# Splitting the feed-forward's first gate slabs anew in each block instead of storing the parts

## Chip, cores, metric

The kernel runs on one core of a Trainium2 chip. The metric is the device time of one execution in microseconds (us), median of several runs.

## What is computed

One layer of a hybrid encoder, in float32, for a prompt of 2048 tokens and a sample of 64 tokens (2112 rows), with a model width of 1024. The change sits between the last residual of the attention part and the feed-forward:

```python
x = x + gt1 * (merged @ p['w_o'])

h2 = rms_norm(x, p['norm2_g']) * (1 + sc2) + sh2
gate, up = jnp.split(h2 @ p['w_ffn_in'], 2, axis=-1)
x = x + gt2 * ((jax.nn.silu(gate) * up) @ p['w_ffn_out'])
```

Before it stand an adaLN-conditioned norm, one input projection, a convolution module and band attention in parallel, and their gated merge. The hidden width of the feed-forward is 2816, 22 slices f of 128.

## The kernel before, in words

**Precision.** Each float32 factor of a product is split into a high part, rounded to the reduced format fp32r, and a low part, the rest. A product is three matmuls: high by high, high by low, low by high. For a weight slab ScalarE (ACT) makes the high part by a copy into `whi`, and VectorE (DVE) or GpSimd (POOL) the low part `wlo` by a subtraction.

**Stages.** The tokens go through the feed-forward in three blocks s = 0, 1, 2 of 576, 768 and 768 rows (`CBLOCKS`). Each is worked in two halves of 288 or 384 rows. In each block, merge (`ca` slabs) and output projection (`wo` slabs) come first; then, tile by tile of 128 tokens, the residual: VectorE forms `x`, ACT its sum of squares (`xn<-x`, the "square"), POOL `r`, the reciprocal root, ACT scales (`xn<-x,r`), TensorE (PE) transposes (`pw<-ident,xn`), and ACT and DVE apply the conditioning and make the operands of the feed-forward: `b` (b11, b21, b22), sums `t` (t1 to t4), each with a high and a low part. The feed-forward's products are arranged in a Strassen-like scheme: some operands are sums of slices of the weights (`s1` to `s4`, made on POOL from raw slabs as `ws`, and kept in DRAM as `sum_d` for the later blocks), others are the raw slices. Several products `early` and `tg` are taken ahead of time.

**The slabs of the change.** The keys `("fi", f*P)` for the first five f (`EARLY = 5`) are raw gate slabs of 128 x 8 x 128, 512 KB each. They feed the first products of the first half (`first(f)` and `second(f)`, lines 2216 to 2240; `ps<-b,whi` in the profile), which TensorE starts while the other tiles are still in the residual: 24 products each, 120 in all. In block 0 the raw slab is loaded (`load`, L375) into a staging buffer (`wst`, three; `wup`, one more) and split in two parts of 4 x 128 columns (`split`, L451): the copies on ACT, the subtractions on VectorE for odd f and on POOL for even f (`turn`). After the split, `then` stores both parts to DRAM (`w_dfi_h`, `w_dfi_l`, L501). In blocks 1 and 2 nothing is split: `split` finds the key in `self.stored` and loads both parts straight into `whi` and `wlo` (L466). Five buffers of each (`held`) go round among all slabs.

**What sets the order.** Each engine works through its own queue in the order of issue. A planner (`stream`) writes that order as the program is built: work is put in lanes with estimated loads of the engines, and a step that has become due is issued where the estimate says so. Loads go out on SyncE's queue (SP) as staging buffers come free by the same estimate (`load_on`, `drop`); sums are formed when their raw slabs should have landed (`presum`). So an edit to one slab can move others' places in the queues.

The order of slabs (lines 584 to 608): per block `ca` and `wo` for each half, then the five `fi`, then pairs of sums and raw slices (`up`), and the down projection's (`dn`, `fo`).

Of the kernel before, what the change touches and what calls it, by code (L numbers as in the profile page):

```python
# [57 lines left out]
SCORE_ROOM = {"dve": 2500}  # L58
TURN_NS = 600.0
POOL_BEHIND = 3000.0  # L60
KEPT = ("qkv", "in", "fi")
EARLY = 5


# [519 lines left out]
def weight_order():  # L584
    yield from (("qkv", 0, k) for k in range(4))
    for b, stage in ORDER:
        if stage == "g":
            for g in range(0, 16, 2):
                yield from (("in", 2560 + g * P, h) for h in range(2))
        elif stage in ("q", "k", "v"):  # L590
            if b or stage != "q":
                yield from (("qkv", "qkv".index(stage), k) for k in range(4))
        else:
            yield from (("in", CONV + stage * P), ("in", stage * P))
    for s in range(len(CBLOCKS)):
        for _ in range(2):
            yield from (("ca", c) for c in range(KT))
            yield from (("wo", k) for k in range(KT))
        yield from (("fi", f * P) for f in range(EARLY))
        for f in range(0, NF, 2):  # L600
            ops = up_operands(f) + up_operands(f + 1)
            for j in range(0, len(ops), 2):
                yield ("up", *ops[j : j + 2])
                if f >= 2 and seven(s, f - 2):
                    yield from (("dn", s, f - 2, *DOWN_OPERANDS[i]) for i in {0: (0,), 2: (1, 2), 4: (3,)}.get(j, ()))
                elif j == 0 and f >= 2 and f - 2 not in last_rows(s):
                    yield from (("fo", f - 2), ("fo", f - 1))
        yield from (("fo", f) for f in last_rows(s))
# [3 lines left out]
def streaming_layer(ctx: ExitStack, tc: tile.TileContext, I, O):  # L612
# [294 lines left out]
    def first_rows():  # L907
        places = ((wa, "x", 3), (wa, "x", 3), (wa, "x", 3), (wk, "kk", 1), (wk, "q2", 1))
        queues = (nc.sync, nc.sync, nc.scalar, nc.sync, nc.scalar)
        return [load_x(*tl, *place, q) for tl, place, q in zip(token_tiles(*PBLOCKS[0]), places, queues)]  # L910
# [691 lines left out]
    xs = first_rows()  # L1602
    W = Weights((nc.sync, act, dve, gps), wpool, dram, stream, list(weight_order()), source, 3, 5, lambda key: key[0] in KEPT)
    first_block(xs)
# [692 lines left out]
```

## Time and profile before

| | |
|---|---|
| median of 3 runs | 2979.57 us (2976.84 to 2982.91) |
| the profiled execution | 2979.5 us |
| its span | 2977.7 us |
| mean granted TensorE clock | 0.995 |
| PE busy | 2900.2 us (97%) |
| DVE busy | 2025.9 us (68%) |
| ACT busy | 1356.8 us (46%) |
| POOL busy | 1127.7 us (38%) |
| DMA | 628.05 MB, 211 GB/s on average |

The profile is of one execution, and its times are us from the span's start. A row of the timeline gives the start, the length, the engine, the line of the code, the operation, the tile written and the tiles read, the size, and in brackets how long the engine had stood idle before it and on whose result. A row of groups gives the count, the summed busy time, the mean in ns, and the idle time before. Starts that follow each other by less than the length of the first belong to operations that overlap in the engine's pipeline. Nearly all compute instructions carry L102, a helper that records them, so they are told apart by their tiles. The feed-forward of block 0 begins near 1307 us, of block 1 near 1851 us, of block 2 near 2480 us.

### The profile page before, as it was taken

The numbers are of one execution on the slowest core, as the hardware profiler recorded it, in microseconds if no ns is written. First come the engines' busy times: TensorE is split into PE (matmuls) and PEld (weight loads), VectorE is DVE, ScalarE is ACT, GpSimd is POOL, SyncE is SP. The second block draws the span as 40 slices with busy tenths as digits, with TensorE's granted clock in tenths as the row PEclk, the third lists the DMA queues.
The fourth block names the chain that finished last, engine by engine and source line by source line (L and its number), as shares of the span: only waits on it lengthen the run. The fifth ranks groups of instructions, "written<-read, shape, count | busy, mean of one in ns | idle before, by whom it ended". The sixth has DMA issues, their size and how long they took to land.

```text
span 2977.7 us, 44838 instructions
## 1 busy us (share of the span) xinstructions
PE 2900.2 (97%) x16199; PEld 2593.1 (87%) x16199; DVE 2025.9 (68%) x3637; ACT 1356.8 (46%) x2441; POOL 1127.7 (38%) x727
## 2 busy tenths in 40 slices
PE   7999899999999999989999999999999999999999
PEld 4899777787888888888999999999999999999998
DVE  5797677767856886577777755666666557466666
ACT  2345642662456257464444345534444345344442
POOL 0201310111011102454466443255666741465667
PEclk9999999999999999999999999999999999999999
DMA  8889889878987798885444786333333975333333
GB/s 290 300 286 310 270 279 312 284 251 274 306 283 224 267 263 278 262 288 175 145 145 159 244 263 235 116 95 106 114 113 113 316 239 184 93 95 114 114 103 128
DMA packets 467723, 628.05 MB, mean 211 GB/s; under 512 B 36276, under 2 KB 314664, under 8 KB 467501
## 3 DMA queue, kind: packets, MB, share of 16 engines
q1 hardware_dynamic: 453456, 605.58, 62.8%
q10 hardware_dynamic: 14045, 19.60, 1.9%
q8 instruction: 127, 2.08, 0.3%
q14 instruction: 95, 0.78, 0.1%
HBM read 476.53 MB, written 148.54 MB: 210 GB/s over the span
## 4 chain that ended last, share of the span: by engine, by line
PE 82%; DVE 7%; DMA 4%; ACT 2%; issue 2%; POOL 2%; SPq 0%; ACTq 0%; POOLq 0%; DVEq 0%
PE ps L102 53%; PE pd L102 16%; PE pw L102 6%; DVE y L102 2%; PE sc L102 2%; PE po L102 2%; PE ptp L102 2%; DVE wlo L102 1%; PE pt L102 1%; DMA kk<-k_d 1%; ACT whi L102 1%; PE pa L102 1%; POOL r L102 1%; DVE pw L102 1%; DMA wst<-in_w_in 0%
## 5 line engine op out<-in xcount | busy, mean ns | idle before, releaser
L102 PE MATMUL ps<-t,whi 128*128 128x384 f32 (+1 forms) x2112 | 503.1, 322 | 8.7 <-ACT t L102 4.9
L102 POOL TENSOR_TENSOR wlo<-wst,whi 128x1024 fp32r<-128x1024 f32 (+1 forms) x156 | 356.4, 2294 | 279.0 <-ACT whi L102 262.6
L102 ACT ACTIVATE whi<-wst 128x1024 fp32r<-128x1024 f32 (+1 forms) x263 | 256.8, 979 | 331.2 <-PE ps L102 119.8
L102 PE MATMUL ps<-b,whi 128*128 128x384 f32 (+1 forms) x1584 | 381.7, 326 | 7.0 <-DVE early L102 3.6
L102 PEld LDWEIGHTS ps<-t,whi 128*128 128x128 f32 x2112 | 367.8, 188 | 16.3 <-ACT t L102 5.1
L102 DVE SCALAR_TENSOR_TENSOR y<-u,wd,y 128x512 f32<-128x512 f32 (+1 forms) x480 | 369.0, 773 | 6.3
L102 PE MATMUL ps<-hh,whi 128*128 128x512 f32 (+2 forms) x992 | 361.7, 365 | 0.0
L102 DVE TENSOR_TENSOR acc<-acc,pd 128x512 f32<-128x512 f32 x464 | 311.7, 685 | 62.7 <-PE pd L102 60.2
L102 PE MATMUL ps<-hl,whi 128*128 128x512 f32 (+2 forms) x992 | 345.6, 348 | 0.0
L102 PE MATMUL ps<-hh,wlo 128*128 128x512 f32 (+2 forms) x992 | 345.4, 348 | 0.0
L102 PE MATMUL ps<-t,wlo 128*128 128x384 f32 (+1 forms) x1056 | 339.4, 322 | 0.8 <-POOL wlo L102 0.7
L102 PE MATMUL pd<-whi,hid 128*128 128x512 f32 x972 | 314.8, 390 | 0.0
L102 PEld LDWEIGHTS ps<-b,whi 128*128 128x128 f32 x1584 | 278.7, 189 | 13.1 <-DVE early L102 4.5
L102 POOL TENSOR_TENSOR r<-t,mhalf 128x1 f32<-128x1 f32 (+3 forms) x68 | 83.6, 1232 | 462.1 <-DVE t L102 457.0
L102 PE MATMUL ps<-b,wlo 128*128 128x384 f32 (+1 forms) x792 | 257.3, 325 | 0.0
L102 ACT ACTIVATE pr<-pr,sm 128x640 f32<-128x640 f32 (+3 forms) x272 | 200.1, 747 | 112.1 <-DVE sm L102 109.5
L102 PEld LDWEIGHTS pd<-whi,hid 128*128 128x128 f32 x972 | 182.5, 188 | 37.7 <-ACT hid L102 0.7
L102 PEld LDWEIGHTS ps<-hh,wlo 128*128 128x128 f32 x992 | 186.7, 188 | 21.6
L102 PEld LDWEIGHTS ps<-hh,whi 128*128 128x128 f32 x992 | 187.2, 189 | 18.5 <-issue 1.6
L102 PEld LDWEIGHTS ps<-hl,whi 128*128 128x128 f32 x992 | 187.5, 189 | 15.5 <-issue 1.4
L102 PEld LDWEIGHTS ps<-t,wlo 128*128 128x128 f32 x1056 | 198.2, 188 | 2.2 <-POOL wlo L102 1.3
L102 PE MATMUL pd<-wlo,hid 128*128 128x512 f32 x508 | 198.6, 391 | 0.0
(226 smaller groups left out, 6170.6 us busy)
## 6 DMA issues: line engine op xcount, KB each, us to landing
whi<-w_din_h SPq DMA_DIRECT2D x72, 512.0 KB, 6.5
wlo<-w_din_l SPq DMA_DIRECT2D x72, 512.0 KB, 8.4
wst<-sum_d SPq DMA_DIRECT2D x132, 256.0 KB, 2.7
wfo<-in_w_ffn_out SPq DMA_DIRECT2D x64, 512.0 KB, 3.2
wmod<-in_w_ada SPq DMA_DIRECT2D x46, 512.0 KB, 6.5
sum_d<-ws SPq DMA_DIRECT2D x88, 256.0 KB, 2.8
wst<-in_w_ffn_in SPq DMA_DIRECT2D x84, 256.0 KB, 3.1
wst<-in_w_in SPq DMA_DIRECT2D x40, 512.0 KB, 8.8
```

The lines of the kernel that those rows point to most:

```text
L102: self.last = f(*args, **kw)
```

## The change

`KEPT` names the kinds of slabs whose split parts are stored in DRAM at their first use and loaded again afterwards. `fi` is taken off the list. In block 0 the ten stores (five high, five low parts) go. In blocks 1 and 2 each `fi` slab is loaded raw into a staging buffer and split there as in block 0. The planner makes the orders of the queues anew.

```diff
@@ -58,7 +58,7 @@
 SCORE_ROOM = {"dve": 2500}
 TURN_NS = 600.0
 POOL_BEHIND = 3000.0
-KEPT = ("qkv", "in", "fi")
+KEPT = ("qkv", "in")
 EARLY = 5
```

The lines that it switches:

```python
W = Weights((nc.sync, act, dve, gps), wpool, dram, stream, list(weight_order()), source, 3, 5, lambda key: key[0] in KEPT)
...
if key in self.again and key not in self.stored and not passing:
    ds = [self.dram.tile(shape, F32, name="w_d" + "_".join(map(str, key)) + "_" + part) for part in "hl"]
    for t, d in zip((hi, lo), ds):
        self.sync.dma_start(d, t.bitcast(F32))
    self.stored[key] = ds, shape
```

## Prediction

> **What bounds the kernel now.** I read the page first, then its times by stage, then single instructions where the change acts. Of the page, the busy times and the chain that ended last:
>
> ```profile
> PE 2900.2 (97%) x16199; PEld 2593.1 (87%) x16199; DVE 2025.9 (68%) x3637; ACT 1356.8 (46%) x2441; POOL 1127.7 (38%) x727
> PE 82%; DVE 7%; DMA 4%; ACT 2%; issue 2%; POOL 2%; SPq 0%; ACTq 0%; POOLq 0%; DVEq 0%
> ```
>
> TensorE has 77.5 of 2977.7 us free, so a microsecond in which it newly waits is a microsecond of time, and none is made good later. The shares say little of the change, which acts at three places only: where each token block goes from its residual into the feed-forward. The table of stretches (us, then busy PE, PEld, DVE, ACT, POOL, PE clock, DMA share, GB/s) shows them for block 1, and one row of block 2:
>
> ```profile
> 1820.00:1840.00 20.00, 20.00 (x90) 16.58 (x89) 3.61 (x5) 3.18 (x3) 3.57 (x2) 1.00 0.48 159
> 1840.00:1860.00 20.00, 19.84 (x105) 17.64 (x105) 14.81 (x30) 13.45 (x28) 1.65 (x3) 1.00 0.72 261
> 1860.00:1880.00 20.00, 19.20 (x111) 18.48 (x110) 19.97 (x33) 14.89 (x27) 5.81 (x2) 1.00 0.33 113
> 2490.00:2510.00 20.00, 19.29 (x111) 18.89 (x112) 19.31 (x31) 13.85 (x25) 5.70 (x2) 1.00 0.33 108
> ```
>
> Over the whole run VectorE is busy 68%; from 1860 to 1880 it is busy 19.97 of 20 us, and TensorE is still 96% busy. There the two are level. That is the stage that prices the change, and it has no room on VectorE. Before 1840 all the helpers are nearly idle, and work that can move there is free. TensorE loses only 0.96 us in the two windows 1840 to 1880, so blocks 1 and 2 can win about 2 us together and no more.
>
> **What the change takes away.** All moves of the split slabs stand on SP's queue:
>
> ```profile
> L466 SPq DMA_DIRECT2D whi<-w_dfi_h x10: 319/383/498, 1834.3 to 2480.2; - x10
> L501 SPq DMA_DIRECT2D w_dfi_h<-whi x5: 531/1115/3045, 1298.8 to 1317.9; - x5
> ```
>
> With the low parts there are 10 stores in block 0 and 10 loads in each of blocks 1 and 2, each 512 KB. The stores go; the 20 loads become 10 loads of raw slabs, so SP issues 20 DMAs fewer. In blocks 1 and 2 DMA is at 0.33 to 0.72, and no wait of TensorE there hangs on a load; the saved bytes are worth nothing there.
>
> **What it adds.** In blocks 1 and 2 each of five slabs is split in two halves of 512 columns: ten ACT copies per block, four subtractions on VectorE (slabs 1 and 3), six on GpSimd (slabs 0, 2, 4). Block 0 already does this work, and gives the durations:
>
> ```profile
> L102 ACT ACTIVATE whi<-wst 128x512 fp32r<-128x512 f32 x50 | 30.9, 625 | 24.2 <-issue 18.2 <-POOL wlo L102 2.9 <-PE ps L102 2.9
> L102 DVE TENSOR_TENSOR wlo<-wst,whi 128x512 fp32r<-128x512 f32 x28 | 33.0, 1185 | 7.9 <-ACT whi L102 7.0 <-PE ps L102 0.5
> L102 POOL TENSOR_TENSOR wlo<-wst,whi 128x512 fp32r<-128x512 f32 x22 | 33.1, 1505 | 6.9 <-ACT whi L102 6.9
> ```
>
> So 10 x 0.63 = 6.3 us on ACT, 6 x 1.5 = 9.0 on GpSimd, 4 x 1.19 = 4.7 on VectorE at these means. VectorE's mean is raised by neighbours: alone the operation takes 0.68, beside a running GpSimd sum 1.76. GpSimd's own shortest of this size is near 1.27.
>
> ```profile
> 1333.07 0.68 DVE L102 TENSOR_TENSOR wlo<-wst,whi 128x512 fp32r<-128x512 f32 x1
> 1342.93 1.76 DVE L102 TENSOR_TENSOR wlo<-ws,whi 128x512 fp32r<-128x512 f32 x1
> 1327.91 1.27 POOL L102 TENSOR_TENSOR ws<-wst 128x512 f32<-128x512 f32 x1 [10.48 <-DVE t L102]
> ```
>
> [...]
>
> What part is on the path follows from the built order of the changed program, which is the same in blocks 1 and 2. ACT has slab 0's two copies ahead of tile 0's square (there it sat idle 10.33 us: free, and so are GpSimd's two halves). Then come slabs 1 to 4, mixed into the work on the three token tiles of the residual: slabs 3 and 4 between the square of tile 1 and its scaling. GpSimd has the four halves of slabs 2 and 4 ahead of the small r (root of the mean square) of tiles 1 and 2. VectorE has slab 1 and 3 amid tile 0's columns. In the timeline of block 1 before:
>
> ```profile
> 1841.48 1.06 ACT L102 ACTIVATE xn<-x 128x1024 f32<-128x1024 f32 x1 [10.33 <-DVE x L102]
> 1848.01 1.07 ACT L102 ACTIVATE xn<-x 128x1024 f32<-128x1024 f32 x1
> 1849.43 0.55 POOL L102 TENSOR_TENSOR r<-t,mhalf 128x1 f32<-128x1 f32 x1 [5.99 <-DVE t L102]
> 1850.01 1.16 ACT L102 ACTIVATE xn<-x,r 128x1024 f32<-128x1024 f32 x1 [0.50 <-POOL r L102]
> 1851.13 0.52 PE L102 MATMUL ps<-b,whi 128*128 128x384 f32 x2
> 1851.66 0.52 PE L102 MATMUL ps<-b,whi 128*128 128x384 f32 x2
> 1853.26 1.03 PE L102 MATMUL pw<-ident,xn 128*128 128x128 f32 x8
> 1854.05 0.60 PE L102 MATMUL ps<-b,whi 128*128 128x384 f32 x2
> 1863.77 1.04 PE L102 MATMUL pw<-ident,xn 128*128 128x128 f32 x8
> 1875.24 0.52 PE L102 MATMUL ps<-t,whi 128*128 128x384 f32 x2
> ```
>
> Step 1, the norm of tile 1. Back to back an ACT copy takes some 0.5 (0.63 less an overlap of 0.1). Four more (slabs 1 and 2) stand ahead of the square, which goes from 1848.0 to 1850.0 and ends at 1851.1; slab 4's buffer, the one of the last output-projection slab, comes free just then, at 1851.13. Four copies more (slabs 3 and 4) end near 1853.1. GpSimd's two halves of slab 4 follow the copies, from 1852.6, and at 1.27 each end near 1855.4 with the hand-over; r comes at 1856 instead of 1849.98, 6.0 later. Tile 1 is scaled by 1857.2 instead of 1851.2.
>
> Step 2, TensorE. Before, tile 1 was transposed at 1853.26, after 12 of the 120 gate products, and tile 2 at 1863.77, after 60; in the built order after, both stand behind the 60th. A product takes (1851.66 - 1851.13) / 3 = 0.177, so 60 take 10.6; with an estimated 0.8 of waits for the gate banks they end at 1862.55, the transposes (1854.05 - 1853.26 = 0.8 a tile) at 1864.15, and the other 60 at 1874.8. The delay of r is thus mostly hidden on TensorE itself: it does products meanwhile. What isn't hidden is VectorE, which had done tile 1's columns in that time.
>
> Step 3, VectorE.
>
> ```profile
> 1847.81 0.41 DVE L102 TENSOR_SCALAR xn<-pw,A,B 128x128 f32<-128x128 f32 x1 [0.61 <-ACT xn L102]
> 1867.97 0.68 DVE L102 TENSOR_TENSOR pw<-pw,b 128x512 f32<-128x512 f32 x1
> 1868.57 0.40 DVE L102 TENSOR_SCALAR pw<-pw,A,B 128x128 f32<-128x128 f32 x1
> 1868.89 0.39 DVE L102 TENSOR_SCALAR xn<-pw,A,B 128x128 f32<-128x128 f32 x1
> 1874.24 0.68 DVE L102 TENSOR_TENSOR t<-pw,t 128x512 fp32r<-128x512 f32 x1
> 1874.83 1.22 DVE L102 TENSOR_TENSOR wlo<-wup,whi 128x1024 fp32r<-128x1024 f32 x1
> 1875.97 0.69 DVE L102 TENSOR_TENSOR pw<-xn,pw 128x512 f32<-128x512 f32 x1
> 1881.27 0.56 DVE L102 TENSOR_TENSOR u<-ps,early 128x384 f32<-128x384 f32 x1 [0.76 <-PE ps L102]
> ```
>
> From start to start an operation of 512 columns takes 0.60, one of 128 columns 0.32, a subtraction of 1024 columns 1.14. After the first transposes (1863.35) the built order has 14 of 512 and 6 of 128 up to the last tile's t3: 10.3 us. The columns go to and fro with ACT; the wait of 0.61 shows such a hand-over, and I allow four or five, 2.7. The t3 is ready at 1876.4, which TensorE wants at 1874.8: 1.6 late, where it came in time before. From there to u, whose end frees the bank for the next products, stand 9 of 512, two of 1024, and three gate operations (0.46, the 0.56 of u less 0.1 of overlap): 9.1 us, so u starts at 1885.5, against 1881.27: 4.2 late. In between TensorE has 24 products and 12 more (6.4 us), which, with 0.8 of waiting for the next t, last until 1883.6; then it waits some 2.3 for u. I take 4.2 us per block.
>
> Bounds of a block: below, -1 (the waits TensorE has now); 0 if VectorE's idle takes the halves up; 1.6 if only the t3 wait shows. Above, the delay of r passed on whole (6.0) with 2.4 of halves, 8.4. I take 4.2 because it lies nearest to VectorE's own rows, which leave it no idle in this stretch.
>
> **Block 0.** TensorE stands three times here, and after the first two the clock is low:
>
> ```profile
> 1318.72 0.73 PE L102 MATMUL ps<-b,whi 128*128 128x288 f32 x2 [2.63 <-DVE early L102]
> 1319.49 0.68 PE L102 MATMUL ps<-b,whi 128*128 128x288 f32 x2
> 1320.21 0.68 PE L102 MATMUL ps<-b,whi 128*128 128x288 f32 x2
> 1321.41 0.44 PE L102 MATMUL ps<-b,wlo 128*128 128x288 f32 x1
> 1322.85 0.42 PE L102 MATMUL ps<-b,whi 128*128 128x288 f32 x2
> 1323.25 0.43 PE L102 MATMUL ps<-b,whi 128*128 128x288 f32 x2
> 1329.06 0.58 PE L102 MATMUL ps<-t,whi 128*128 128x288 f32 x1 [4.85 <-ACT t L102]
> 1345.11 0.54 PE L102 MATMUL ps<-t,whi 128*128 128x288 f32 x2 [1.59 <-DVE u L102]
> ```
>
> Three products take 0.72 after the wait of 2.63 and 0.40 later; the 12 from 1318.72 to 1321.41 so cost 1.3 us more. GpSimd's sum at 1327.91 (quoted above) had stood idle for 10.48 us; VectorE's t that the profile names was long done, and what is late is a store of earlier sums, which SP could issue only behind the last L501 stores, after 1319. Without these the sums can come some 6 to 8 us earlier. But the 2.63 and the 4.85 hang on VectorE's and ACT's column work, which isn't waiting for a sum; only the 1.59 comes behind subtractions that run beside late sums (the 1.76 above). Against that, the built order has one ACT copy of a sum (0.5) ahead of the columns. So between -1.6 and +0.5; I take -0.5. If I have the first two waits wrong, the whole stretch can give up to 2.63 + 4.85 + 1.59 + 2 x 1.3 = 11.7.
>
> The sum: 2 x 4.2 - 0.5 = +7.9, on the profiled execution's 2979.5 (span 2977.7 and 1.8 around it), which is the median 2979.57 of the runs to 0.1: **2987.4 us**.
>
> **Rivals.** *Nothing measurable.* VectorE's halves slip into the idle of 1840 to 1860 (it was free 5.2 of 20 us) and TensorE's waits only change places: 0 to 2 per block, 2979 to 2983. For it: TensorE runs 60 products ahead without tile 1. Against it: 19.97 of 20.
>
> *Faster.* One mechanism: in block 0 the store queue, not the columns, is what feeds the 4.85 and 1.59 waits. With the sums 8 us earlier these go, and one slow-clock stretch with them: 4.85 + 1.59 + 1.3 = -7.7, and with 0.5 per block elsewhere 2972.8. It decides only if the blocks cost under 1.7 us together. For it: DMA is dense there and 10 of SP's issues go. Against: the releasers named, ACT t and DVE early.
>
> *Much slower.* The waits in blocks 1 and 2 (1.6 and 2.3) grow past the point at which the clock drops. It lies between 1.59, after which products weren't slow, and 2.63, after which they were. Then 1.3 per wait, and 4.2 becomes 5.5 to 6.8; if two halves also run beside GpSimd, 2 x (1.76 - 0.68) = 2.2 more, up to 8: from 2990 to 2995. [...]
>
> *The change does nothing* (loads kept): the built order has no store and no reload of these slabs; I give it no chance.
>
> **Numbers.** My forecast (2984 to 2991) 0.50, much slower 0.20, nothing measurable 0.20, faster 0.10. A difference of 0.2%, 6 us, is what a measurement of this kernel can tell. So the first and second count as slower, but for 0.05 at the low end of mine (under 2985.5), which goes to the same: slower 0.65, same 0.25, faster 0.10. Range 2975 to 2997: it takes in the second bound of the blocks (the much slower case) and the low end of the case without effect, and leaves out most of the faster case.
>
> **What would show it.** In block 1 after: r of tile 1 some 5 us after the first gate product instead of 1.2 before it, behind GpSimd's four halves; tiles 1 and 2 transposed together; TensorE's waits before the first t product and for u, together near 4; VectorE full to u. In block 0: GpSimd's sums earlier, the waits of 2.63 and 4.85 still there. I am wrong if TensorE's busy share of the 40 us after 1840 stays above 97%, if block 0 loses its 4.85, or if VectorE shows idle ahead of u.

## The result, and the profile after

The changed kernel takes 2998.23 us (median of 4 runs, 2991.70 to 3000.19) against 2980.22 before: a ratio of 1.0061 (95% interval 1.0048 to 1.0074), 18 us slower. The forecast was 7.9 us slower, 2987.4, with a range to 2997. The profiled execution has a span of 2998.4 us, 20.7 longer. Busy times of the page after:

```profile
PE 2906.6 (97%) x16199; PEld 2595.6 (87%) x16199; DVE 2039.8 (68%) x3649; ACT 1367.8 (46%) x2461; POOL 1134.4 (38%) x735
```

VectorE, ACT and GpSimd have 13.9, 11.0 and 6.7 us more to do, in 12, 20 and 8 more instructions (the splits are eight on VectorE and twelve on GpSimd; the planner also gave VectorE four later subtractions that GpSimd had before); TensorE has the same matmuls and 20.7 - 6.4 = 14.3 us more of idle time. Where that lies is seen when the same matmuls are set beside each other in both traces: how much later (us) a matmul starts, as the median over a stretch. It is 1.8 before the feed-forward of block 0 (nothing that the change touches; other runs are up to 5.5 us early there), 2.3 after it, 3.2 ahead of block 1's residual, 11.5 after block 1's first gates, 13.0 ahead of block 2's residual and 21.1 from there to the end. Block 1 loses 8.3, block 2 8.1, block 0 0.5; the other 2.4 come in steps near 1750 and 2340 us, where runs without any split have steps too. "Shift" below means this difference over the place in block 1 and in block 2.

The stretches that answer to those of before:

```profile
1840.00:1860.00 20.00, 20.00 (x101) 17.60 (x101) 14.43 (x24) 10.74 (x21) 7.39 (x7) 1.00 0.52 162
1860.00:1880.00 20.00, 18.21 (x106) 17.08 (x104) 17.59 (x31) 18.43 (x36) 3.34 (x3) 1.00 0.36 129
1880.00:1900.00 20.00, 14.68 (x73) 14.00 (x74) 16.03 (x24) 6.18 (x9) 2.39 (x1) 0.91 0.33 105
2510.00:2530.00 20.00, 15.48 (x78) 14.55 (x77) 18.80 (x30) 13.14 (x25) 2.40 (x1) 0.91 0.17 53
```

TensorE now loses most in the third stretch, where it lost nothing before, and its clock is at 0.91 there. TensorE's timeline of block 1 after:

```profile
1861.99 0.62 PE L102 MATMUL ps<-b,whi 128*128 128x384 f32 x2 [1.16 <-ACT early L102]
1864.49 0.62 PE L102 MATMUL ps<-b,whi 128*128 128x384 f32 x2 [0.29 <-DVE early L102]
1866.90 1.91 PE L102 MATMUL pw<-ident,xn 128*128 128x128 f32 x16
1881.26 0.45 PE L102 MATMUL ps<-t,whi 128*128 128x384 f32 x1 [1.60 <-DVE t L102]
1886.38 0.98 PE L102 MATMUL ps<-t,whi 128*128 128x384 f32 x2 [2.94 <-DVE early L102]
1887.48 0.84 PE L102 MATMUL ps<-t,whi 128*128 128x384 f32 x2
1888.44 0.84 PE L102 MATMUL ps<-t,whi 128*128 128x384 f32 x2
1892.87 0.62 PE L102 MATMUL ps<-t,whi 128*128 128x384 f32 x2 [1.12 <-DVE early L102]
```

Tiles 1 and 2 are transposed together (16 transposes in one row), as the built order had it. Then come the 1.60 for t3, and 2.94 and 1.12 for gate operations of VectorE. After the 2.94 three products take 0.96 instead of 0.53 (1887.48 to 1888.44), for nine products: 1.3 us. The five waits are 7.1, before they were 1.0; with the clock 7.4 of the 8.3 are found.

The last of them is for the gate operation right ahead of u, the operation of VectorE at which the prediction's working ends. What holds u up (VectorE, GpSimd, ACT):

```profile
1882.32 1.66 DVE L102 TENSOR_TENSOR b<-xn,b 128x512 fp32r<-128x512 f32 x1
1891.67 0.69 DVE L102 TENSOR_TENSOR t<-pw,t 128x512 fp32r<-128x512 f32 x1 [1.50 <-ACT t L102]
1892.74 0.55 DVE L102 TENSOR_TENSOR u<-ps,early 128x384 f32<-128x384 f32 x1
1881.04 2.39 POOL L102 TENSOR_TENSOR wlo<-wst,whi 128x1024 fp32r<-128x1024 f32 x1 [13.70 <-ACT whi L102]
1890.09 1.06 ACT L102 ACTIVATE whi<-wup 128x1024 fp32r<-128x1024 f32 x1 [3.25 <-PE ps L102]
```

Less the shift of 3.2, u starts at 1889.5, 8.3 later than before. VectorE's `b` takes 1.66 beside GpSimd's subtraction (0.68 at 1874.22, with GpSimd idle). Then VectorE stands 1.50 for ACT's `t`, which comes behind a copy, and the copy waits for TensorE's slow products.

On the other engines, at the place of the norm of tile 1 (GpSimd, VectorE, ACT):

```profile
1853.35 2.88 POOL L102 TENSOR_TENSOR wlo<-wup,whi 128x512 fp32r<-128x512 f32 x2 [6.72 <-issue]
1856.46 3.18 POOL L102 TENSOR_TENSOR wlo<-wst,whi 128x512 fp32r<-128x512 f32 x2 [0.24 <-POOL wlo L102]
1859.83 0.55 POOL L102 TENSOR_TENSOR r<-t,mhalf 128x1 f32<-128x1 f32 x1 [0.18 <-DVE t L102]
1855.52 2.97 DVE L102 TENSOR_TENSOR wlo<-wst,whi 128x512 fp32r<-128x512 f32 x2
1859.61 0.14 DVE L102 TENSOR_SCALAR t<-ssq 128x1 f32<-128x1 f32 x1
1865.92 1.97 DVE L102 TENSOR_TENSOR b<-xn,b 128x512 fp32r<-128x512 f32 x1
1860.41 1.15 ACT L102 ACTIVATE xn<-x,r 128x1024 f32<-128x1024 f32 x1 [2.18 <-POOL r L102]
```

Two halves on VectorE (slab 3) take 2.97, at the 0.68 of a lone one and a spacing of 0.60 it would be 1.3; they run beside GpSimd's, which are slowed too (3.18 for two; a lone one takes 1.30 in the run with all low parts on GpSimd, below). The two of slab 1 met none and took 0.69 and 0.68. A single `b` operation takes 1.97 beside a GpSimd subtraction. Summed over block 1's gates (65 us), VectorE's instructions take 4.4 us more than the short durations of the same instructions (their tenth percentile over the runs), against 1.3 in the kernel before. This sum is called VectorE's excess below.

### The profile page after: what moved, and what is told of

It reads as the page before. It is cut to its first block, busy times and chain, and to the rows that moved or that the text cites. A ratio compares the mean times of both kernels' runs of the same rounds, so it can differ in the third digit from the quotient of the medians.

```text
span 2998.4 us, 44840 instructions
## 1 busy us (share of the span) xinstructions
PE 2906.6 (97%) x16199; PEld 2595.6 (87%) x16199; DVE 2039.8 (68%) x3649; ACT 1367.8 (46%) x2461; POOL 1134.4 (38%) x735
## 4 chain that ended last, share of the span: by engine, by line
PE 78%; DVE 8%; DMA 6%; ACT 3%; issue 2%; POOL 2%; SPq 0%; ACTq 0%; DVEq 0%; POOLq 0%
PE ps L102 50%; PE pd L102 15%; PE pw L102 5%; DVE y L102 2%; PE sc L102 2%; PE po L102 2%; PE ptp L102 2%; DVE wlo L102 2%; ACT whi L102 1%; PE pt L102 1%; PE pa L102 1%; DVE pw L102 1%; POOL r L102 1%; DMA wst<-in_w_in 1%; POOL wlo L102 1%
## 5 line engine op out<-in xcount | busy, mean ns | idle before, releaser
L102 ACT ACTIVATE whi<-wst 128x1024 fp32r<-128x1024 f32 (+1 forms) x277 | 264.8, 962 | 357.6 <-PE ps L102 116.0
L102 DVE TENSOR_TENSOR wlo<-wst,whi 128x1024 fp32r<-128x1024 f32 (+1 forms) x117 | 143.8, 1233 | 100.8 <-ACT whi L102 99.6
```

The lines of the kernel that those rows point to most:

```text
L102: self.last = f(*args, **kw)
```

## The experiments

Theory: the splits in blocks 1 and 2 cost the time, by VectorE's own time, by two engines that hold each other up (a subtraction on VectorE took 1.76 beside a GpSimd sum, 0.68 alone), and by tile 1's place in the order. Rivals: the stores or loads; r of tile 1 behind GpSimd; ACT's copies; the order alone. All times are medians, with the ratio to the kernel before on the same chip and its 95% interval.

**Stores kept, not read.** In `then`, besides:

```diff
+if key[0] == "fi" and i == self.keys.index(key):
+    for t, part in ((hi, "h"), (lo, "l")):
+        self.sync.dma_start(self.dram.tile(shape, F32, name=f"w_x{key[1]}_{part}"), t.bitcast(F32))
```

> The changed kernel, but block 0 still stores both parts of the five slabs (10 stores of 512 KB); nothing reads them, and blocks 1 and 2 split anew. Theory (the cost is the work of splitting in blocks 1 and 2; the stores cost nothing): same as the changed kernel, 2994 to 3001. Rival A (the stores were worth time in block 0 by holding SP's queue and DMA): slower than the changed kernel by over 4 us, above 3002. Rival B (something that the stores' absence moved in the planner's order cost time): below 2990.

2992.63 us, ratio 1.0054 (1.0039 to 1.0069), shift 6.9 and 8.3. Just under the theory's band, but the interval overlaps that of the changed kernel, and neither rival's time came. This run also prices the slow clock. In block 1 its queues of TensorE, VectorE and ACT hold the same work in the same order as the changed kernel's, and the wait of 2.94 is there, but the products behind it run at full clock (TensorE, ACT, VectorE):

```profile
1883.80 0.59 PE L102 MATMUL ps<-t,whi 128*128 128x384 f32 x2 [2.94 <-DVE early L102]
1884.40 0.51 PE L102 MATMUL ps<-t,whi 128*128 128x384 f32 x2
1886.04 1.06 ACT L102 ACTIVATE whi<-wup 128x1024 fp32r<-128x1024 f32 x1 [1.77 <-PE ps L102]
1888.68 0.55 DVE L102 TENSOR_TENSOR u<-ps,early 128x384 f32<-128x384 f32 x1
```

ACT's copy waits 1.77 instead of 3.25, VectorE no longer stands ahead of u, and u is 6.8 late (less its shift of 0.6) instead of 8.3. The slow clock was worth 1.4 of block 1's 8.3.

**No stores, no splits.** The kernel before with

```diff
+if key[0] == "fi":
+    ds = next(d for k, (d, s) in self.stored.items() if k[0] == "in" and list(s) == list(shape))
+else:
     for t, d in zip((hi, lo), ds):
         self.sync.dma_start(d, t.bitcast(F32))
```

> The kernel before without the 10 stores of block 0; blocks 1 and 2 load parts of the same shape from another stored slab (so the numbers of these products are another slab's) and split nothing. Theory: as before, 2977 to 2983. Rival A (relief of block 0 by the missing stores): 2972 or less. Rival B (loss from the missing stores or the new order): above 2986.

2978.53 us, ratio 1.0002 (0.9992 to 1.0011), shift 0.1 and 0.0, and 0.3 in block 0. The 5.2 MB of stores are worth nothing; block 0 is no part of the result.

**ACT's copies alone, and the subtractions alone.** In `split`, for `fi` in blocks 1 and 2, `tensor_tensor` or `activation` gives way to a load:

```diff
+if key[0] == "fi" and i > self.keys.index(key):
+    if c.start == 0:
+        self.sync.dma_start(lo.bitcast(F32), other[1])   # the second kernel: hi, other[0], in place of the copy
+    continue   # the first kernel alone
```

Here `other` stands for the stored parts of a slab `in` of the same shape.

> The changed kernel, but in blocks 1 and 2 the low parts are not computed: they are loaded from another stored slab (other numbers); the raw loads and ACT's ten copies per block stay, the four subtractions on VectorE and the six on GpSimd go. [...] Rival (the raw loads in the staging buffers or ACT's copies are the cost): 2993 or more.

> The changed kernel, but in blocks 1 and 2 the high parts are loaded from another stored slab (other numbers) and ACT makes no copies; the raw loads and the subtractions on VectorE and GpSimd stay. Theory: r of tile 1 still stands behind GpSimd and VectorE is still full, so half of the loss or more stays, 2987 to 2996. Rival (ACT's copies ahead of tile 1's square are the cost): 2979 to 2984.

Copies alone: 2986.02 us, ratio 1.0031 (1.0021 to 1.0041), shift 3.6 and 2.7. In the band on record for the theory, 2980 to 2987, by which most of the loss goes without the subtractions; but two fifths of the shift and nearly half of the time stay, with no low part computed. Subtractions alone: 2994.70, ratio 1.0063 (1.0046 to 1.0080), shift 8.5 and 6.6. As expected in time, but not for the reason given: r of tile 1 came ahead of GpSimd's halves there and was not late (1846.26, less the shift of -3.2 the 1849.43 of before). It tells little, since GpSimd waited 7.4 us for the load of a high part in the midst of the tiles, a wait that the changed kernel hasn't, and TensorE's order is another one (tile 1 transposed behind 36 products, tile 2 behind 113).

The copies alone have TensorE's order of the changed kernel as to the tiles (both behind 60 products). So the next two part the order from the work.

**The order without the work, the work without the order.** First, in the kernel before, on the path that loads stored parts; second, in the changed kernel, around the splits:

```diff
+if key[0] == "fi":
+    name, ns = ("dve", 607.0) if key[1] // P % 2 else ("pool", 1212.0)
+    load = self.stream.load
+    for _ in range(2):
+        load["act"] = max(load["act"], load["pe"]) + 645.0
+        self.stream.after(name, "act")
+        load[name] = max(load[name], load["pe"]) + ns
...
+charged = dict(self.stream.load)
 for c, src in parts:
...
+if key[0] == "fi" and i > self.keys.index(key):
+    self.stream.load.update(charged)
```

> The kernel before in its work (parts stored in block 0, loaded in blocks 1 and 2, nothing split there), but the planner is charged for the five slabs in blocks 1 and 2 as if it split them (per half 645 ns on ACT, and 607 on VectorE or 1212 on GpSimd). The queues then come out as in the changed kernel: tile 1 is transposed with tile 2 behind 60 gate products instead of alone behind 12. Theory O (the place of tile 1 in the order is over half of the loss): 4 to 5 us per block, 2986 to 2991. Theory W (the engines' time for the splits is the loss): 2976 to 2982.

> The changed kernel with all of its splits, but the planner isn't charged for the five slabs' splits in blocks 1 and 2, so the queues stand nearly as before (tile 1 transposed behind 14 gate products, tile 2 behind 60) with the copies and subtractions put in. Theory O: the loss shrinks to what the four halves on VectorE and ACT's copies cost, 1 to 3 us per block, 2981 to 2986. Theory W: 2993 to 3000 as the changed kernel.

Order only: 2985.44 us, ratio 1.0021 (1.0012 to 1.0030), shift 2.9 and 3.5. Work only: 2986.98, ratio 1.0022 (1.0012 to 1.0033), shift 3.2 and 3.2. TensorE's timeline of the first (two rows) and of the second (three rows), block 1:

```profile
1860.22 1.91 PE L102 MATMUL pw<-ident,xn 128*128 128x128 f32 x16
1876.82 0.58 PE L102 MATMUL ps<-t,whi 128*128 128x384 f32 x2 [1.97 <-DVE early L102]
```

```profile
1856.26 1.09 PE L102 MATMUL pw<-ident,xn 128*128 128x128 f32 x8 [1.47 <-ACT xn L102]
1860.08 0.62 PE L102 MATMUL ps<-b,whi 128*128 128x384 f32 x2 [0.96 <-ACT early L102]
1865.92 0.62 PE L102 MATMUL ps<-b,whi 128*128 128x384 f32 x2 [1.33 <-DVE early L102]
```

A kernel that splits nothing loses 3.2 us per block because the planner believes that it does: with both tiles' columns left to the end, VectorE comes late for the gates. A kernel that splits everything in nearly the old order loses as much, at other places: the norm of tile 1 behind ACT's copies, the banks (the `ps` tiles) of the gate products. Neither theory is right alone; 6.4 of the 8.2 are the sum of the two, each of about the same size. They differ in one thing: the order alone has a stretch of slow clock in each block (TensorE's mean clock is 0.91 from 1870 to 1890 and from 2500 to 2520), the work alone has none there (1.00).

**Slab 0 alone.** `KEPT` with the key of slabs 1 to 4:

```diff
-lambda key: key[0] in KEPT)
+lambda key: key[0] in KEPT or key[0] == "fi" and key[1] // P in (1, 2, 3, 4))
```

> Only slab 0 is split anew in blocks 1 and 2 (slabs 1 to 4 are stored and loaded as before). Its copies and GpSimd's two halves fall where ACT had been idle 10.33 us. Both theories: hidden, 2976 to 2982. Rival (any raw load or split at this place costs): 1.5 us per block or more, above 2983.

2982.49 us, ratio 1.0012 (1.0003 to 1.0022), shift 3.3 and 1.6: in time between the two bands, by the shift the rival's size, though the split did fall into ACT's idle time. (Block 1 has slow products behind the wait, three in 0.96 us from 1877.20, and block 2 has none: 3.3 against 1.6.) The trace shows why. VectorE, GpSimd and TensorE of this run, then GpSimd of the kernel before:

```profile
1870.78 3.42 DVE L102 TENSOR_TENSOR wlo<-wst,whi 128x1024 fp32r<-128x1024 f32 x1
1870.73 2.40 POOL L102 TENSOR_TENSOR wlo<-wst,whi 128x1024 fp32r<-128x1024 f32 x1 [11.34 <-ACT whi L102]
1875.42 0.77 PE L102 MATMUL ps<-t,whi 128*128 128x384 f32 x3 [2.03 <-DVE early L102]
```

```profile
1874.89 3.42 POOL L102 TENSOR_TENSOR wlo<-wst,whi 128x1024 fp32r<-128x1024 f32 x1 [11.45 <-ACT whi L102]
```

Before, VectorE's subtraction began at 1874.83 (shown in the prediction), took 1.22, and GpSimd's, 0.06 later, took 3.42. Here GpSimd is 0.05 ahead, takes 2.40, and VectorE's takes 3.42. In both traces the subtraction that began second took 3.42. Here it is VectorE's, 2.2 us longer than before, and TensorE waits 2.03 behind it. To test that, GpSimd alone gets a small operation more, once in each of blocks 1 and 2, ahead of this subtraction (the condition that picks it out isn't shown); the queues of all other engines stay:

```diff
+self.gps.tensor_tensor(lo[:, 0, :1], src[:, 0, :1], hi[:, 0, :1].bitcast(F32), ALU.subtract)
 e.tensor_tensor(lo[:, c], src, hi[:, c].bitcast(F32), ALU.subtract)
```

> Slab 0 alone split anew, as in the earlier run of it, in which TensorE waited 2.0 us in each of blocks 1 and 2 for a gate operation of VectorE; VectorE's 1024-column subtraction before that had taken 3.42 us there, started 0.05 us after one on GpSimd (1.22 in the kernel before, where VectorE started 0.06 us ahead of GpSimd). Here GpSimd alone gets one more operation, of 128x1, right before its subtraction; the queues of all other engines are the same. Theory P (whichever engine starts second of two subtractions in SBUF waits for the other): VectorE is back at 1.2, the 2.0 wait goes, 4 to 5 us less than that run's blocks, 2976 to 2981. Rival (the long subtraction has another cause, or GpSimd is the one waited for): the wait stays or moves, 2981 to 2985.

2976.95 us, ratio 0.9993 (0.9983 to 1.0002), shift 0.1 and 0.1. The loss is gone, by added work. VectorE and GpSimd (whose row holds the small operation and the large one):

```profile
1874.04 1.21 DVE L102 TENSOR_TENSOR wlo<-wst,whi 128x1024 fp32r<-128x1024 f32 x1
1873.97 3.54 POOL L102 TENSOR_TENSOR wlo<-wst,whi 128x1 fp32r<-128x1 f32 x2 [11.33 <-ACT whi L102]
```

So the split of slab 0 itself is hidden, and so is its raw load.

**Which engine has the low parts.** Only slabs 2 and 4 anew (GpSimd), only slabs 1 and 3 (VectorE), by the other keys in `KEPT` as for slab 0; then all five, with the low parts of blocks 1 and 2 all on GpSimd, or all on VectorE:

```diff
-"fi": key[1] // P if key[0] == "fi" else 0
+"fi": 0 if i > self.keys.index(key) else key[1] // P if key[0] == "fi" else 0   # 0: all on GpSimd, 1: all on VectorE
```

> Only slabs 2 and 4 are split anew in blocks 1 and 2 (low parts on GpSimd; no halves on VectorE). Tile 1 is transposed behind 36 gate products, tile 2 behind 78 of the 120. If r behind GpSimd's four halves and ACT's four copies is what counts: 2 to 4 us per block, 2983 to 2988. If VectorE's own halves are the cost: 2977 to 2982.

> Only slabs 1 and 3 split anew in blocks 1 and 2: four halves on VectorE, none on GpSimd. TensorE's order is the same as with slabs 2 and 4 alone, which cost 4.3 us per block. Theory (VectorE is full, so its own 2.4 us add to what the order costs): 4 to 6 per block, 2987 to 2993. Rival (GpSimd ahead of r was the cost with slabs 2 and 4): 1 to 2 per block, 2980 to 2984.

> All five slabs split anew, with all low parts of blocks 1 and 2 on GpSimd. TensorE's order is that of the run with ACT's copies alone (3.1 us per block there). [...] Rival (r of tile 1 behind GpSimd's halves is the rest): eight halves ahead of it, 8 or more per block, above 2994.

> All five slabs split anew, with all low parts of blocks 1 and 2 on VectorE: eight halves in the full stretch instead of four (2.4 us more), nothing on GpSimd ahead of r, no GpSimd half beside them. TensorE transposes tile 1 behind 60 products. [...]

| | us | ratio (95%) | shift, us |
|---|---|---|---|
| slabs 2, 4 (GpSimd) | 2986.06 | 1.0023 (1.0013 to 1.0033) | 3.8, 4.9 |
| slabs 1, 3 (VectorE) | 2986.14 | 1.0026 (1.0016 to 1.0035) | 4.9, 3.7 |
| all, on GpSimd | 2985.11 | 1.0026 (1.0017 to 1.0036) | 4.4, 3.4 |
| all, on VectorE | 2991.08 | 1.0044 (1.0029 to 1.0059) | 5.5, 5.4 |
| all, on both (the change) | 2998.23 | 1.0061 (1.0048 to 1.0074) | 8.3, 8.1 |

All of these four but the second fell into the band that its reason gave, the second just under it. (For all on GpSimd that was 2985 to 2992, if the rest of the loss is VectorE's halves and their waits; for all on VectorE 2986 to 2994, if r and the meeting of the two engines cost more than the 2.4 of four halves more, and 2998 to 3006 if VectorE's time alone counts.) But the traces show that two of the assumptions did not hold. With slabs 2 and 4, r of tile 1 came ahead of GpSimd's halves and was not late:

```profile
1849.85 0.55 POOL L102 TENSOR_TENSOR r<-t,mhalf 128x1 f32<-128x1 f32 x1 [5.98 <-DVE t L102]
1850.58 2.57 POOL L102 TENSOR_TENSOR wlo<-wst,whi 128x512 fp32r<-128x512 f32 x2 [0.18 <-POOL r L102]
```

And TensorE's order was not the same in the first two runs: tiles 1 and 2 stand together behind 60 products with slabs 2 and 4, and behind 36 and 102 with slabs 1 and 3. Their 4.3 us each thus don't compare the engines. With all low parts on GpSimd the tiles stand as in the change and as in the copies alone, both behind 60. Five halves then stand ahead of r of tile 1 and three more ahead of tile 2's, and r of tile 1 is 5.6 late; yet the loss is 3.9 per block for the change's 8.2 (VectorE's excess is 1.7 to 1.8 per block, 4.4 in the change):

```profile
1848.91 1.30 POOL L102 TENSOR_TENSOR wlo<-wst,whi 128x512 fp32r<-128x512 f32 x1
1850.17 0.55 POOL L102 TENSOR_TENSOR r<-t,mhalf 128x1 f32<-128x1 f32 x1
1850.69 3.80 POOL L102 TENSOR_TENSOR wlo<-wst,whi 128x512 fp32r<-128x512 f32 x3
```

That is 0.8 per block more than the copies alone in the same order, so r behind GpSimd's halves is nearly free, and the rival named for that falls. With the tiles behind the same 60 products four runs make a ladder, per block: the order alone 3.2, with ACT's copies 3.1, with all low parts on GpSimd 3.9, and 8.2 with slabs 1 and 3 on VectorE. So more than half of the loss comes with VectorE's four halves: their own 2.4, 2.7 more of VectorE's excess, and the longer waits behind them. All on VectorE puts four halves more into its full stretch (2.4 us) and is still 2.8 per block cheaper by the shift, though the intervals of the two ratios overlap. Its order differs as well: TensorE transposes tile 2 behind 80 products there. What the mixed form has over both is that the two engines subtract at once; that this is the whole difference is shown for neither.

## Why the prediction was wrong

**The step that failed** is the last leg of Step 3, from the t3 to u: it took VectorE's operations at their lone spacing and TensorE at full clock, so that u would come 4.2 late. Both terms were put at nothing, and u came 8.3 late; the blocks measured 8.3 and 8.1. Of the 4.1 more, 2.5 arose in this leg and 1.6 before it. The sign and the place were right. Piece by piece:

- *The terms of the sum.* Blocks 1 and 2: +8.4 forecast, +16.4 measured. Block 0: -0.5 forecast, +0.5 in the trace and 0.3 without stores and splits; nothing.
- *Step 1.* r came 7.2 late, by the start of its row less the shift of 3.2, for a forecast of 6.0; it waited in the end for VectorE's t, which stood behind VectorE's slowed halves. The run with GpSimd alone shows that a delay of r is not what costs most.
- *Step 2.* Behind the 60th product, as read from the order. The banks' waits were 1.45 for 0.8: the longer one is for ACT's `early`, which stood behind the late scaling of tile 1. The transposes start at 1863.7 less the shift, for 1862.55.
- *Step 3 up to the t3.* The wait is 1.60 for 1.6, and that is luck in part: both ends of it came 1.6 to 1.7 later than worked out (wanted at 1876.5 for 1874.8, ready at 1878.0 for 1876.4, less the shift).
- *Step 3 from the t3 to u.* Here it fails: 9.1 forecast, 11.5 measured, and waits of 0.8 and 2.3 became 2.94 and 1.12 with slow products in between. Of the 2.4 more, 1.0 is the `b` beside GpSimd's subtraction (1.66, and 1.58 to the next start instead of 0.60), and 1.5 is VectorE's wait for ACT behind the slow products, which isn't there in block 1 of the run with stores, where the clock stayed up. VectorE's row for a GpSimd neighbour (1.76 for 0.68) was quoted, but the sum counted each operation at 0.60 and left the meeting, and the clock, to a rival. Two halves did meet GpSimd's, for 1.7; that shows in r above. A change of GpSimd's start alone is worth 4.8 us over two blocks, slow clock in one of them included. The runs show what a meeting costs, 1.22 or 3.42 by who is first; no run shows by what the two engines hold each other up.
- *Rivals.* "Much slower" came nearest: GpSimd's neighbourhood and the clock together, up to 8 per block, with a chance of 0.20. Its price of the clock, 1.3 per wait, was right, with one wait per block instead of two; its 2990 to 2995 still lay below the measured time. "Nothing measurable" (the idle before 1860) and "faster" (block 0) fell: the sums of block 0 do come early, and TensorE's waits there don't shrink.

GpSimd in block 0 after, and TensorE:

```profile
1321.16 1.28 POOL L102 TENSOR_TENSOR ws<-wst 128x512 f32<-128x512 f32 x1 [1.95 <-DVE pw L102]
1320.49 0.54 PE L102 MATMUL ps<-b,whi 128*128 128x288 f32 x2 [2.62 <-DVE early L102]
1321.00 0.42 PE L102 MATMUL ps<-b,whi 128*128 128x288 f32 x2
1321.39 0.42 PE L102 MATMUL ps<-b,whi 128*128 128x288 f32 x2
1330.59 0.61 PE L102 MATMUL ps<-t,whi 128*128 128x288 f32 x1 [5.90 <-ACT t L102]
```

The first sum starts 6.8 earlier than before (1327.91), as forecast. The 2.62 stayed, the 4.85 became 5.90.

What stays open: of the 8.2, order and work, each measured without the other, make 6.4, so that 1.8 come only when they meet (by the ratios some 5 of 18 us, no more than the three intervals together leave unsure). VectorE's excess is 3.1 us more than before, enough for that, and 4.3 of the 8.2 come with VectorE's four halves; but no run took the collisions alone out of the changed kernel. For block 2 no run of the same work kept the clock up, so its price there isn't measured.

## What to carry to other kernels

When work is added to a stretch where an engine is full, price it at the duration beside its neighbour, not alone: here, of two subtractions of 1024 columns that VectorE and GpSimd began within 0.06 us, the first took 1.22 (VectorE) or 2.40 (GpSimd) and the second 3.42, so the engine nearest to the path should come first or have them alone. An edit to a kernel whose queues are planned by estimates has two prices, the work and the order that the estimate makes of it; they can be measured apart by charging the planner without the work, and the other way round. A difference of a few us between two versions may hang on which of two instructions starts 0.05 us earlier, so look for one long duration before giving the edit the blame. A reason can be wrong where its time comes out right: read from the trace whether the queues came out as the experiment assumed.

## What was not expected of the hardware

A wait of 2.63 us in block 0 was followed by slow products before; the wait of 2.62 at the same place in the trace after was not (three products in 0.39, 1321.00 to 1321.39). The 2.94 of block 1 was followed by slow products in the changed kernel and by none in the run with stores. So the length of a wait doesn't settle by itself whether the clock drops. How the two differ can be read from the granted clock: in these traces it changes at moments that lie 3.41 us, or a multiple of it, apart. TensorE's busy time and clock in such stretches, before (two rows), after (two rows) and with the stores (two rows); behind the clock stand DMA's share and GB/s:

```profile
1315.51:1318.92 3.41, 0.78 (x7) 0.99 1.08 396
1318.92:1322.33 3.41, 3.15 (x13) 0.50 1.02 393
1882.80:1886.21 3.41, 0.65 (x4) 1.00 0.00 0
1886.21:1889.62 3.41, 3.23 (x10) 0.50 0.13 23
1882.01:1885.42 3.41, 1.62 (x9) 1.00 0.00 0
1885.42:1888.83 3.41, 2.52 (x14) 1.00 0.70 178
```

TensorE stood 2.63 and 2.76 us of the first and third stretch, and the next was at half clock. With the stores the same 2.94 was cut by the end of a stretch, 1.79 fell into this one, and the clock stayed. The 2.62 after was cut as well: TensorE stood 1.70 us of the stretch from 1316.16 to 1319.57 and 1.31 of the next, both at full clock. In the traces of before and after, a stretch at full clock with 1.9 us or more of standing was followed by half clock each time (13 of 13), one with less than 1.8 almost never (2 of 1697). So the same wait can fall within one stretch or be cut by its end, and in these two traces 1.9 of 3.41 us were enough.

A subtraction of 1024 columns on VectorE took 3.42 us behind one on GpSimd that had begun 0.05 us earlier, as if it had not been let in until the other ended: 2.35 to that end, and 1.07 from there, near its own 1.22.
